# Inverse roots of the norms as one GpSimd power instruction, and a rope step of VectorE placed later

## The chip, the cores and the metric

The program runs on one core of a Trainium2 chip. The metric is the device time of one execution in microseconds (us), the median of several runs. TensorE (PE) multiplies matrices into PSUM, VectorE (DVE), ScalarE (ACT) and GpSimd (POOL) do elementwise work, and SyncE (SP) issues most of the loads. Each engine works through its own queue of instructions in order; an instruction that waits for another engine holds up everything behind it in its queue.

## The reference

Two layers of a decoder trunk on 256 tokens of width 1024. Each layer has three token mixers side by side, then a SwiGLU block and a gated embedding; each part begins with an RMSNorm.

```
def rmsnorm(x, g):
    y = xf * lax.rsqrt(jnp.mean(xf * xf, axis=-1, keepdims=True) + EPS)
    return (y * g)
per layer:
  h = rmsnorm(x); z = h @ W_in              # split into q, k, v, ... of mixers A, B, C
  A: sparse attention, B: sliding window with sinks, C: latent attention
     (C: rmsnorm of the low-rank q and kv before their up-projections)
  q and k of A and B, part of q and k of C: rotated by cos/sin(position * frequency)
  x += (sum of sigmoid(h @ Wg_i) * (o_i @ Wp_i)) @ W_out
  x += SwiGLU(rmsnorm(x));  x += sigmoid(rmsnorm(x) @ W_pg) * (p @ W_pe)
out = rmsnorm(x)
```

Two things of it matter here: the inverse square root, one number for each token and norm (256 numbers for each of seven norms of x, 512 for each layer's two low-rank norms together), and the rope tables, sine and cosine of position times frequency, which are made once.

## The kernel before

The 256 tokens are two tiles of 128 (t = 0, 1), tokens on partitions. Every product with a weight is made by `lin` in three float32r matmuls (high part of the input by high and by low part of the weight, low part by high part). So each weight chunk of up to 1024 columns is loaded by SP (tile `raw`, four buffers), rounded by ScalarE into `wh`, and the remainder taken by VectorE into `wl` (`wl<-raw,wh`); six pairs `wh`, `wl` are held. A full chunk serves 12 matmuls of 128x512, six for each token tile.

A norm of x does not scale its input: `Norm.tr` (or `parts` at the start) transposes x on TensorE, VectorE multiplies by the gain (`xg`), ScalarE rounds to the high part and VectorE makes the low part (both in tile `hT`). ScalarE meanwhile sums the squares (`junk`, into `ssq`). The inverse root `nm.r[t]` is needed only when a finished product leaves PSUM: as the scale of ScalarE's instruction, or as half of it (`rh`) in tanh for a sigmoid. The function `newton` makes the root: GpSimd adds the two halves of `ssq` and EPS (tile `n0v` or `n1v`, for t = 0 or 1), VectorE makes a first guess on the bits (`n0y`, `n1y`), and GpSimd does three Newton steps of two instructions (`n0a`, `n0y`), or of four for the low-rank norms of C (`c0v`, `c0y`, `c0a`, two columns). Of the last norm, t = 1 alone runs on VectorE, and `finish` then multiplies the output tile `xf` by the root and sends it out.

The first products are the gate of C (`gc0`, chunks 0 to 3, evacuated into `gateC` with `rh`) and the low-rank projections (`g1`, chunks 4 to 7, evacuated into `zc` with `nm.r`, and transposed on TensorE soon after). `lin` has three PSUM banks and takes two for each product, so `g1` for t = 1 reuses the bank that `gateC` of t = 0 frees.

The order on each queue is fixed by the program: a planner (`Plan`) with estimated costs holds small steps back in a list (`W.push`) and emits them between matmuls when they are due. The rope angles are made on GpSimd at the start (`setup_rope`, `rope_parts`, `finish_rope`: tiles `ang`, `kq`, `kp`); `rope_rest` then has VectorE take the larger of the angle and its negative (`kq<-kq,ang`), GpSimd turn it into the cosine's argument, ScalarE take two sines (tile `cs`; each change to or from the sine loads a table) and GpSimd spread them (`tabs`). During the first product, `start_1` and `start_2` emit the second half of the norm's input.

Of the kernel before, what the change touches and what calls it, by code (L numbers as in the profile page):

```python
# [11 lines left out]
I32 = mybir.dt.int32  # L12
AF = mybir.ActivationFunctionType
ALU = mybir.AluOpType
# [3 lines left out]
P = 128  # L18
# [199 lines left out]
def build(tc, wst, xin, pin, posn, cst, lpar, fnorm, out):  # L218
# [13 lines left out]
    W = Plan()  # L232
    V, S, T, G = (Engine(W, n, e) for n, e in (("V", nc.vector), ("S", nc.scalar), ("T", nc.tensor), ("G", nc.gpsimd)))

    def sb(shape, dt=F32, name="t", tag=None, bufs=1, p=pool):
        W.clear(tag or name, bufs)
        p = low if (tag or name) in FIRST else p
        t = p.tile(shape, dt, name=name, tag=tag or name, bufs=bufs)
        W.alloc(t.tensor.name, tag or name, bufs)
        return t  # L240

    def ps(tag, name=None):
        n = {"lin": 3, "pv": 1}.get(tag, 2)
        W.clear("ps" + tag, n)
        t = pp.tile([P, 512], F32, name=name or tag, tag=tag, bufs=n)
        W.alloc(t.tensor.name, "ps" + tag, n)
        return t
# [54 lines left out]
    def split_to(n):  # L302
        st["goal"] = max(st["goal"], n)
        feed()
# [101 lines left out]
    def small(n, name, bufs=2, dt=F32):  # L406
        return sb([P, n], dt, name=name, bufs=bufs)

    def transpose(o, i):
        T.transpose(o, i, ident)  # L410
# [8 lines left out]
    rope_t = {}  # L419
# [16 lines left out]
    def rope_parts(parts):  # L436
        ang, kq = rope_t["ang"], rope_t["kq"]
        kp = sb([P, 2, 48], name="kp", tag="kall", bufs=3)
        for bits in parts:
            rest = rope_t["rest"]  # L440
            part = rest if bits is None else math.floor(rest * 2 ** bits) / 2 ** bits
            rope_t["rest"] = rest - part
            G.tensor_scalar(out=kp, in0=kq, scalar1=-float(np.float32(part)), scalar2=None, op0=ALU.mult)
            G.tensor_tensor(out=ang, in0=ang, in1=kp, op=ALU.add)

    def finish_rope():
        rope_parts((27, None))
        ang, kq = rope_t["ang"], rope_t["kq"]
        pif = float(np.nextafter(np.float32(math.pi), np.float32(0)))
        G.tensor_scalar(out=ang, in0=ang, scalar1=pif, scalar2=-pif, op0=ALU.min, op1=ALU.max)  # L450
        G.tensor_scalar(out=kq, in0=ang, scalar1=-1.0, scalar2=None, op0=ALU.mult)
        W.push([kq], lambda: rope_rest(kq, ang), 0.2, [ang])

    def rope_rest(kq, ang):
        cs = sb([P, 2, 2, 48], name="cs", tag="dup0")
        V.tensor_tensor(out=kq, in0=kq, in1=ang, op=ALU.max)
        G.tensor_scalar(out=kq, in0=kq, scalar1=-1.0, scalar2=float(math.pi / 2), op0=ALU.mult, op1=ALU.add)

        def sin():
            S.activation(out=cs[:, 0], in_=kq, func=AF.Sin)  # L460
            S.activation(out=cs[:, 1], in_=ang, func=AF.Sin)
            W.push([cs], lambda: setup_tabs(cs))
        W.push([kq], sin, 0.2, [ang])

    def setup_tabs(cs):
        for i in range(2):
            for t in range(2):
                G.tensor_copy(out=tabs[:, t, 64 * i:64 * i + 64].rearrange("p (a b) -> p a b", a=2),
                              in_=cs[:, i, t, None, 0:32].to_broadcast([P, 2, 32]))
                G.tensor_copy(out=tabs[:, t, 128 + 32 * i:160 + 32 * i].rearrange("p (a b) -> p a b", a=2),  # L470
                              in_=cs[:, i, t, None, 32:48].to_broadcast([P, 2, 16]))
        ready_set.add("tabs")


    def newton(ssq, n, tag, G=G):

        v, y, a = small(n, tag + "v"), small(n, tag + "y"), small(n, tag + "a")
        one, two = ssq if isinstance(ssq, tuple) else (ssq, None)
        if two is None:
            G.tensor_scalar(out=v, in0=one, scalar1=EPS, scalar2=None, op0=ALU.add)  # L480
        else:
            G.tensor_scalar(out=v, in0=one, scalar1=two, scalar2=EPS, op0=ALU.add, op1=ALU.add)
        V.tensor_scalar(out=y.bitcast(I32), in0=v.bitcast(I32), scalar1=-0.5, scalar2=float(0x5F3759DF),
                        op0=ALU.mult, op1=ALU.add)
        G.tensor_scalar(out=v, in0=v, scalar1=-0.5, scalar2=None, op0=ALU.mult)
        for _ in range(3):
            if n == 1:
                G.tensor_scalar(out=a, in0=y, scalar1=y, scalar2=v, op0=ALU.mult, op1=ALU.mult)
                G.tensor_scalar(out=y, in0=a, scalar1=1.5, scalar2=y, op0=ALU.add, op1=ALU.mult)
            else:  # L490
                G.tensor_tensor(out=a, in0=y, in1=y, op=ALU.mult)
                G.tensor_tensor(out=a, in0=a, in1=v, op=ALU.mult)
                G.tensor_scalar(out=a, in0=a, scalar1=1.5, scalar2=None, op0=ALU.add)
                G.tensor_tensor(out=y, in0=y, in1=a, op=ALU.mult)
        return y

    def split_evac(src_ps, n, hi, lo, then, gain=None):

        s3 = src_ps[:, :n * P].rearrange("p (a b) -> p a b", a=n)
        if gain is not None:  # L500
            xg = sb([P, 4, P], name="xg")
            V.tensor_tensor(out=xg[:, :n], in0=s3, in1=gain[:, :, None].to_broadcast([P, n, P]), op=ALU.mult)
            s3 = xg[:, :n]
        S.copy(out=hi, in_=s3)

        def rest():
            V.tensor_tensor(out=lo, in0=s3, in1=hi.bitcast(F32), op=ALU.subtract)
            then()
        W.push([hi], rest, 0.0, [s3, lo])
# [3 lines left out]
    def finish(t, r):  # L513

        for g, c in enumerate([slice(0, 512), slice(512, 1024)] if t == 0 else [slice(0, 384), slice(384, 1024)]):
            o = xf[t][:, c]
            if g and t:
                V.tensor_scalar(out=o, in0=o, scalar1=r, scalar2=None, op0=ALU.mult)
            else:
                S.activation(out=o, in_=o, func=AF.Copy, scale=r)  # L520
            (nc.sync if g or not t else nc.scalar).dma_start(out=out[0, t * P:(t + 1) * P, c], in_=o)
        sent.append(t)
# [3 lines left out]
    class Norm:  # L526
# [55 lines left out]
            return o  # L582

        def fin(self, t, i=1):
            self.r[t] = newton((self.ssq[t][:, 0:1], self.ssq[t][:, i:i + 1]), 1, f"n{t}",
                               V if self.last and t else G)
            if self.last:
                if t:
                    finish(t, self.r[t])
                return  # L590
            self.rh[t] = small(1, f"rh{t}")
            G.tensor_scalar(out=self.rh[t], in0=self.r[t], scalar1=0.5, scalar2=None, op0=ALU.mult)
# [17 lines left out]
    def layer(l, nm, nxt):  # L610
# [12 lines left out]
        rc = [None, None]  # L623
        rcs = [small(1, f"rcs{t}") for t in range(2)]

        def ev_g1(t, b):
            zc = sb([P, 512], name="zc")
            S.activation(out=zc, in_=b, func=AF.Copy, scale=nm.r[t])
            s2 = small(2, f"s2{t}")
            for i in range(2):  # L630
                junk = sb([P, 512], BF16, name="junk")
                S.activation(out=junk[:, :256], in_=zc[:, 256 * i:256 * i + 256], func=AF.Square,
                             scale=1.0 / 16, accum_out=s2[:, i:i + 1])

            def tr():
                tb = ps("tr")
                for k in range(4):
                    transpose(tb[:, k * P:(k + 1) * P], zc[:, k * P:(k + 1) * P])
                split_evac(tb, 4, cTh[:, :, t * P:(t + 1) * P], cTl[:, :, t * P:(t + 1) * P],
                           lambda: flags.add(f"cT{t}"), lp[:, L_CN:L_CN + 4])  # L640
                rc[t] = newton(s2, 2, f"c{t}")
                G.tensor_scalar(out=rcs[t], in0=rc[t][:, 0:1], scalar1=float(96 ** -0.5), scalar2=None,
                                op0=ALU.mult)
            W.push([zc], tr)
# [641 lines left out]

    setup_rope()
    finish_rope()

    def parts(t, g):  # L1290
# [14 lines left out]
    def split(i):  # L1305
        if st["split"] == i:
            st["split"] += 1
            upper(i)
        return late.get(i, lambda: None)
# [9 lines left out]
    def start_2():  # L1319
        w3 = split(3)  # L1320
        lo = parts(1, 1)
        w3()
        lo()
        w4 = split(4)
        nm.square(0, 1)
        w4()
        nm.square(1, 1)
        W.push([], setup_masks, 20.0)
        split_to(HLB)

# [116 lines left out]
```

## Time and profile before

| | |
|---|---|
| median of 3 runs | 974.86 us (974.83 to 976.6) |
| profiled execution, its own time | 975.02 us |
| its span, first to last instruction | 973.3 us |
| TensorE busy | 955.2 us (98%), granted clock 0.997 |
| VectorE, ScalarE, GpSimd busy | 668.7, 555.5, 105.1 us |

The profiled execution is 0.16 us above the median and 1.7 us longer than its span. TensorE is busy nearly throughout; its idle time lies in the first 35 us, at a few places of some tenths, and after its last matmul. Busy times of TensorE contain pipelining: a 128x512 matmul is shown with about 0.39 us, but the next one starts 0.23 us after it.

### The profile page before, as it was taken

Reading aid. Unit: us, or ns where it says so; the run is one execution under the profiler, and the core shown is the slowest. Engines: PE = TensorE matmul, PEld = TensorE weight load, DVE = VectorE, ACT = ScalarE, POOL = GpSimd, SP = SyncE. Lnnn points to the kernel's source line nnn. Section 1 sums busy time; section 2 is a strip of 40 time slices with the busy share of each in tenths; the row PEclk is TensorE's granted clock in tenths of the full one; section 3 lists DMA queues with packets and bytes.
Section 4 is the critical chain, followed back from the end, with each engine's and each line's share of the span. In section 5 each row is a group of like instructions: output and inputs, shape, how many; then the busy total and the mean of one; then the engine's idle time right before and its main releaser. Section 6 shows DMA issues by size and latency. Waiting matters only on the chain.

```text
span 973.3 us, 13708 instructions
## 1 busy us (share of the span) xinstructions
PE 955.2 (98%) x4915; PEld 784.0 (81%) x4915; DVE 668.7 (69%) x1070; ACT 555.5 (57%) x1013; POOL 105.1 (11%) x224
## 2 busy tenths in 40 slices
PE   8899999999999999999999999999999999999996
PEld 5688888777888888888878898877788888888885
DVE  5697688658776666645767868876786766665555
ACT  5668767565554444543555686666655544444443
POOL 6700000000030000000454000000001200000032
PEclk9999999999999999999999999999999999999998
DMA  7556634434555655556454664343445555555551
GB/s 262 163 168 203 214 95 145 153 106 142 171 184 186 192 198 182 177 190 195 156 174 148 205 200 158 117 166 130 127 140 167 195 188 191 195 183 184 185 173 44
DMA packets 46596, 164.29 MB, mean 169 GB/s; under 512 B 5504, under 2 KB 5760, under 8 KB 46528
## 3 DMA queue, kind: packets, MB, share of 16 engines
q1 hardware_dynamic: 45648, 161.80, 50.5%
q0 software_dynamic: 448, 1.30, 0.5%
q8 instruction: 39, 0.64, 0.3%
q10 hardware_dynamic: 432, 0.32, 0.1%
q14 instruction: 29, 0.24, 0.1%
HBM read 162.35 MB, written 1.05 MB: 168 GB/s over the span
## 4 chain that ended last, share of the span: by engine, by line
PE 93%; POOL 3%; DVE 2%; issue 1%; ACT 1%; ACTq 0%; DVEq 0%; POOLq 0%
PE lin L214 77%; PE tr L214 6%; PE sc L214 5%; PE pv L214 3%; PE hidps L214 2%; POOL kp L214 0%; POOL n1a L214 0%; POOL n0a L214 0%; DVE wl L214 0%; ACT wh L214 0%; POOL ang L214 0%; DVE um L214 0%; POOL kq L214 0%; POOL n0y L214 0%; POOL n0v L214 0%
## 5 line engine op out<-in xcount | busy, mean ns | idle before, releaser
L214 PE MATMUL lin<-wh,hT 128*128 128x512 f32 (+2 forms) x1600 | 512.9, 389 | 1.6 <-DVE hT L214 0.9
L214 DVE TENSOR_TENSOR wl<-raw,wh 128x1024 fp32r<-128x1024 f32 (+2 forms) x308 | 369.0, 1209 | 91.0 <-ACT wh L214 85.4
L214 ACT CAST wh<-raw 128x1024 fp32r<-128x1024 f32 (+2 forms) x308 | 317.0, 1037 | 133.3 <-PE lin L214 125.4
L214 PEld LDWEIGHTS lin<-wh,hT 128*128 128x128 f32 x1600 | 297.0, 188 | 58.5 <-DVE hT L214 1.7
L214 PE MATMUL lin<-wl,hT 128*128 128x512 f32 (+2 forms) x800 | 305.2, 381 | 2.5 <-DVE wl L214 2.5
L214 PEld LDWEIGHTS lin<-wl,hT 128*128 128x128 f32 x800 | 150.8, 189 | 28.2 <-DVE wl L214 3.2
L214 PE MATMUL lin<-wh,hd 128*128 128x512 f32 x352 | 110.9, 392 | 0.0
L214 PEld LDWEIGHTS lin<-wh,hd 128*128 128x128 f32 x352 | 66.1, 188 | 13.6
L214 POOL TENSOR_SCALAR n0v<-ssq 128x1 f32<-128x1 f32 x7 | 2.5, 358 | 686.8 <-ACT junk L214 686.8
L214 PE MATMUL lin<-wl,hd 128*128 128x512 f32 x176 | 68.5, 389 | 0.0
L214 PE MATMUL lin<-wh,oT 128*128 128x512 f32 x192 | 64.6, 397 | 0.0
L214 ACT ACTIVATE th<-lin,rh 128x256 f32<-128x256 f32 (+1 forms) x52 | 26.2, 504 | 66.3 <-PE lin L214 63.2
L214 ACT ACTIVATE p<-sc,negm 128x256 f32<-128x256 f32 (+1 forms) x128 | 52.7, 426 | 2.7 <-DVE negm L214 2.7
L214 DVE SCALAR_TENSOR_TENSOR th<-th,lin 128x256 f32<-128x256 f32 x44 | 18.4, 419 | 49.9 <-ACT th L214 49.9
L214 DVE TENSOR_REDUCE negm<-sc 128x2 f32<-128x512 f32 (+1 forms) x48 | 33.0, 687 | 27.3 <-PE sc L214 27.1
L214 ACT COPY pT<-tr 128x512 f32<-128x512 f32 x48 | 28.1, 584 | 36.2 <-PE tr L214 36.2
L214 PEld LDWEIGHTS lin<-wh,oT 128*128 128x128 f32 x192 | 36.1, 188 | 7.7 <-issue 0.8
L214 PE MATMUL lin<-wh,mT 128*128 128x512 f32 x128 | 41.4, 395 | 0.0
L214 PEld LDWEIGHTS lin<-wl,hd 128*128 128x128 f32 x176 | 33.1, 188 | 6.7
L214 PE MATMUL lin<-wl,oT 128*128 128x512 f32 x96 | 37.5, 390 | 0.0
L214 ACT CAST hd<-tr 128x256 fp32r<-128x256 f32 x44 | 16.2, 369 | 33.5 <-PE tr L214 33.5
L214 DVE TENSOR_TENSOR p<-p,sm 128x512 f32<-128x512 f32 x48 | 33.2, 692 | 2.1
(226 smaller groups left out, 1070.7 us busy)
## 6 DMA issues: line engine op xcount, KB each, us to landing
raw<-wst SPq DMA_DIRECT2D x296, 512.0 KB, 4.0
raw<-wst SPq DMA_DIRECT2D x8, 312.0 KB, 2.8
raw<-wst SPq DMA_DIRECT2D x4, 384.0 KB, 3.1
x<-xin SPq DMA_DIRECT2D x4, 256.0 KB, 5.9
w<-lpar POOLq DMA_DIRECT2D x2, 256.0 KB, 3.0
pr<-pin POOLq DMA_DIRECT2D x2, 256.0 KB, 3.5
fn<-fnorm SPq DMA_DIRECT2D x1, 512.0 KB, 3.3
out<-xf SPq DMA_DIRECT2D x2, 256.0 KB, 2.0
```

Of the source, the lines that this page charges most:

```text
L214: return fn(*a, **k)
```

## The change

The function `newton` becomes `rsqrt`: GpSimd adds EPS as before and then raises the sum to the power of -0.5 in one tensor_tensor instruction whose second input is a small tile `half` that is filled with -0.5 at the start. The guess on VectorE and the Newton steps are gone, for all norms. The last norm's t = 1 goes through GpSimd as well, where before it stayed on VectorE. The step `rope_rest` is no longer pushed with a due time; it is kept in `rope_t["last"]` and emitted in `start_2`, after the last sum of squares.

```
-        W.push([kq], lambda: rope_rest(kq, ang), 0.2, [ang])
+        rope_t["last"] = lambda: rope_rest(kq, ang)
...
-    def newton(ssq, n, tag, G=G):
+    half = sb([P, 2], name="half")
+    G.memset(half, -0.5)
+    def rsqrt(ssq, n, tag):
-        v, y, a = small(n, tag + "v"), small(n, tag + "y"), small(n, tag + "a")
+        v, y = small(n, tag + "v"), small(n, tag + "y")
...
-        V.tensor_scalar(out=y.bitcast(I32), in0=v.bitcast(I32), scalar1=-0.5, scalar2=float(0x5F3759DF),
-                        op0=ALU.mult, op1=ALU.add)
-        G.tensor_scalar(out=v, in0=v, scalar1=-0.5, scalar2=None, op0=ALU.mult)
-        for _ in range(3):
-            if n == 1:
-                G.tensor_scalar(out=a, in0=y, scalar1=y, scalar2=v, op0=ALU.mult, op1=ALU.mult)
-                G.tensor_scalar(out=y, in0=a, scalar1=1.5, scalar2=y, op0=ALU.add, op1=ALU.mult)
-            else:
...
+        G.tensor_tensor(out=y, in0=v, in1=half[:, 0:n], op=ALU.pow)
...
-            self.r[t] = newton((self.ssq[t][:, 0:1], self.ssq[t][:, i:i + 1]), 1, f"n{t}",
-                               V if self.last and t else G)
+            self.r[t] = rsqrt((self.ssq[t][:, 0:1], self.ssq[t][:, i:i + 1]), 1, f"n{t}")
...
-                rc[t] = newton(s2, 2, f"c{t}")
+                rc[t] = rsqrt(s2, 2, f"c{t}")
...
         nm.square(1, 1)
+        rope_t["last"]()
         W.push([], setup_masks, 20.0)
```

VectorE's queue in the first 30 us, before. The first row is the low part of the third of four pieces of the norm's input, the next `xg` belongs to the fourth.

```order
L214 TENSOR_TENSOR hT<-xg,hT 128x4x128
L214 TENSOR_TENSOR kq<-kq,ang 128x96
L214 TENSOR_TENSOR xg<-tr,lp 128x512
L214 TENSOR_TENSOR wl<-raw,wh 128x1024
L214 TENSOR_TENSOR hT<-xg,hT 128x4x128
L214 TENSOR_TENSOR wl<-raw,wh 128x1024
L214 TENSOR_SCALAR n0y<-n0v 128x1
L214 TENSOR_SCALAR n1y<-n1v 128x1
L214 CAST identb<-con 128x128
L214 CAST identr<-con 128x128
L214 CAST masks<-mload 128x256
L214 TENSOR_TENSOR wl<-raw,wh 128x1024 x5
```

The same place after:

```order
L214 TENSOR_TENSOR hT<-xg,hT 128x4x128
L214 TENSOR_TENSOR xg<-tr,lp 128x512
L214 TENSOR_TENSOR wl<-raw,wh 128x1024
L214 TENSOR_TENSOR hT<-xg,hT 128x4x128
L214 TENSOR_TENSOR wl<-raw,wh 128x1024
L214 TENSOR_TENSOR kq<-kq,ang 128x96
L214 TENSOR_TENSOR wl<-raw,wh 128x1024
L214 CAST identb<-con 128x128
L214 CAST identr<-con 128x128
L214 CAST masks<-mload 128x256
L214 TENSOR_TENSOR wl<-raw,wh 128x1024 x4
```

The rope step has moved behind the fourth `xg`, two weight remainders and the last low part of the norm's input; the two guesses are gone.

GpSimd's queue from the last rope instructions on, after. Before, nine instructions stood for each root and its half in place of these three.

```order
L214 TENSOR_SCALAR ang<-ang 128x96
L214 TENSOR_SCALAR kq<-ang 128x96
L373 DMA w_217<-lpar 128x512
L214 TENSOR_SCALAR kq<-kq 128x96
L214 TENSOR_SCALAR n0v<-ssq_135 128x1
L214 TENSOR_TENSOR n0y<-n0v,half 128x1
L214 TENSOR_SCALAR rh_314<-n0y 128x1
L214 TENSOR_SCALAR n1v<-ssq_136 128x1
L214 TENSOR_TENSOR n1y<-n1v,half 128x1
L214 TENSOR_SCALAR rh_329<-n1y 128x1
```

The roots still stand behind the rope instruction that waits for VectorE (`kq<-kq`), so its later place moves them too.

ScalarE's queue from the end of the sums of squares to `zc`, before:

```order
L214 ACTIVATE junk,ssq_134<-x_106 128x512
L214 ACT_TABLE_LOAD
L214 ACTIVATE cs<-kq 128x96
L214 ACTIVATE cs<-ang 128x96
L214 CAST wh<-raw 128x1024 x3
L214 ACT_TABLE_LOAD
L214 ACTIVATE gateC<-lin,rh_322 128x512
L214 ACTIVATE gateC<-lin,rh_345 128x512
L214 CAST wh<-raw 128x1024 x2
L214 ACTIVATE zc<-lin,n0y 128x512
```

and after:

```order
L214 ACTIVATE junk,ssq_136<-x_106 128x512
L214 CAST wh<-raw 128x1024 x2
L214 ACT_TABLE_LOAD
L214 ACTIVATE cs<-kq 128x96
L214 ACTIVATE cs<-ang 128x96
L214 CAST wh<-raw 128x1024
L214 ACT_TABLE_LOAD
L214 ACTIVATE gateC<-lin,rh_314 128x512
L214 ACTIVATE gateC<-lin,rh_329 128x512
L214 CAST wh<-raw 128x1024 x2
L214 ACTIVATE zc<-lin,n0y 128x512
```

Two of the three weight roundings now stand ahead of the sines and their table load. On TensorE and SP the order of the work is the same in both kernels.

## Rows read from the trace of the kernel before

**Rows 1.** The page: busy times (part 1), and the chain that ended last, by engine (part 4).

```profile
PE 955.2 (98%) x4915; PEld 784.0 (81%) x4915; DVE 668.7 (69%) x1070; ACT 555.5 (57%) x1013; POOL 105.1 (11%) x224
...
PE 93%; POOL 3%; DVE 2%; issue 1%; ACT 1%; ACTq 0%; DVEq 0%; POOLq 0%
```

**Rows 2.** Timeline of TensorE, 17 to 35 us: start, duration, instruction, and in brackets the idle time before it and what ended it.

```profile
17.78 0.39 PE L214 MATMUL lin<-wh,hT 128*128 128x512 f32 x1
18.76 0.50 PE L214 MATMUL lin<-wh,hT 128*128 128x512 f32 x1 [0.60 <-ACT hT L214]
...
19.85 0.74 PE L214 MATMUL lin<-wh,hT 128*128 128x512 f32 x2 [0.35 <-DVE hT L214]
...
26.58 0.50 PE L214 MATMUL lin<-wl,hT 128*128 128x512 f32 x1 [1.18 <-DVE wl L214]
26.92 0.62 PE L214 MATMUL lin<-wh,hT 128*128 128x512 f32 x2
...
31.70 0.39 PE L214 MATMUL lin<-wh,hT 128*128 128x512 f32 x1
34.36 0.66 PE L214 MATMUL tr<-con,zc 128*128 128x128 f32 x4 [2.28 <-ACT zc L214]
```

**Rows 3.** Groups of instructions of TensorE in the window 18.7 to 32.2 us, with their counts, busy time, mean ns, and idle time before them.

```profile
L214 PE MATMUL lin<-wh,hT 128*128 128x512 f32 x32 | 10.3, 398 | 1.0 <-ACT hT L214 0.6 <-DVE hT L214 0.4
L214 PE MATMUL lin<-wl,hT 128*128 128x512 f32 x16 | 6.3, 397 | 1.2 <-DVE wl L214 1.2
```

**Rows 4.** Timeline of VectorE, 14 to 29 us.

```profile
14.27 0.75 DVE L214 TENSOR_TENSOR hT<-xg,hT 128x512 fp32r<-128x512 f32 x1
17.20 0.26 DVE L214 TENSOR_TENSOR kq<-kq,ang 128x96 f32<-128x96 f32 x1 [2.18 <-POOL kq L214]
17.38 0.68 DVE L214 TENSOR_TENSOR xg<-tr,lp 128x512 f32<-128x512 f32 x1
...
19.71 1.22 DVE L214 TENSOR_TENSOR wl<-raw,wh 128x1024 fp32r<-128x1024 f32 x1
...
24.77 0.16 DVE L214 TENSOR_SCALAR n1y<-n1v 128x1 int32<-128x1 int32 x1 [3.47 <-POOL n1v L214]
...
25.31 3.49 DVE L214 TENSOR_TENSOR wl<-raw,wh 128x1024 fp32r<-128x1024 f32 x3
```

**Rows 5.** Timeline of ScalarE, 18 to 34 us.

```profile
18.09 0.62 ACT L214 CAST hT<-xg 128x512 fp32r<-128x512 f32 x1 [3.53 <-DVE xg L214]
...
21.06 1.28 ACT L214 ACT_TABLE_LOAD   x1
...
22.72 2.93 ACT L214 CAST wh<-raw 128x1024 fp32r<-128x1024 f32 x3
25.66 1.28 ACT L214 ACT_TABLE_LOAD   x1
26.95 0.69 ACT L214 ACTIVATE gateC<-lin,rh 128x512 f32<-128x512 f32 x1
31.16 0.69 ACT L214 ACTIVATE gateC<-lin,rh 128x512 f32<-128x512 f32 x1 [3.51 <-POOL rh L214]
...
33.62 0.69 ACT L214 ACTIVATE zc<-lin,n0y 128x512 f32<-128x512 f32 x1
```

**Rows 6.** Timeline of GpSimd, 17 to 37 us.

```profile
17.12 0.62 POOL L373 DMA_DIRECT2D w<-lpar  x1
...
20.38 0.73 POOL L214 TENSOR_SCALAR n0v<-ssq 128x1 f32<-128x1 f32 x1 [2.33 <-ACT junk L214]
...
23.78 0.26 POOL L214 TENSOR_SCALAR n0y<-n0a,n0y 128x1 f32<-128x1 f32 x1
...
25.53 3.31 POOL L214 TENSOR_SCALAR n1a<-n1y,n1v 128x1 f32<-128x1 f32 x1
...
30.91 0.21 POOL L214 TENSOR_SCALAR rh<-n1y 128x1 f32<-128x1 f32 x1
...
36.21 0.20 POOL L214 TENSOR_TENSOR c0a<-c0y 128x2 f32<-128x2 f32 x1
```

**Rows 7.** Timeline at the start of the second layer: VectorE, then TensorE.

```profile
499.55 0.15 DVE L214 TENSOR_SCALAR n1y<-n1v 128x1 int32<-128x1 int32 x1 [3.09 <-POOL n1v L214]
499.62 0.68 DVE L214 TENSOR_TENSOR hT<-xg,hT 128x512 fp32r<-128x512 f32 x1
...
499.47 0.39 PE L214 MATMUL lin<-wl,hT 128*128 128x512 f32 x1
500.36 0.73 PE L214 MATMUL lin<-wh,hT 128*128 128x512 f32 x2 [0.50 <-DVE hT L214]
```

**Rows 8.** Timeline of the end: GpSimd, VectorE, ScalarE.

```profile
962.09 0.29 POOL L214 TENSOR_SCALAR n0v<-ssq 128x1 f32<-128x1 f32 x1 [8.46 <-ACT junk L214]
...
966.84 0.21 DVE L214 TENSOR_SCALAR n1v<-ssq 128x1 f32<-128x1 f32 x1 [0.18 <-ACT junk L214]
...
969.13 0.55 DVE L214 TENSOR_SCALAR xf<-xf,n1y 128x640 f32<-128x640 f32 x1
...
966.62 0.19 ACT L214 ACTIVATION_READ_ACCUMULATOR junk<-x 128x1 f32 x1
967.27 1.33 ACT L214 ACTIVATE xf<-xf,n0y 128x512 f32<-128x512 f32 x2 [0.47 <-POOL n0y L214]
969.13 0.62 ACT L214 ACTIVATE xf<-xf,n1y 128x384 f32<-128x384 f32 x1 [0.53 <-DVE n1y L214]
```

More of the change, by code (lines that the diff above doesn't have):

```diff
@@ L482, in newton @@
             G.tensor_scalar(out=v, in0=one, scalar1=two, scalar2=EPS, op0=ALU.add, op1=ALU.add)
-        V.tensor_scalar(out=y.bitcast(I32), in0=v.bitcast(I32), scalar1=-0.5, scalar2=float(0x5F3759DF),
-                        op0=ALU.mult, op1=ALU.add)
-        G.tensor_scalar(out=v, in0=v, scalar1=-0.5, scalar2=None, op0=ALU.mult)
-        for _ in range(3):
-            if n == 1:
-                G.tensor_scalar(out=a, in0=y, scalar1=y, scalar2=v, op0=ALU.mult, op1=ALU.mult)
-                G.tensor_scalar(out=y, in0=a, scalar1=1.5, scalar2=y, op0=ALU.add, op1=ALU.mult)
-            else:
[L491 to L494, printed above, removed]
+        G.tensor_tensor(out=y, in0=v, in1=half[:, 0:n], op=ALU.pow)
         return y
```

## The prediction

> **What bounds the kernel now.** I read the page's busy times and chain first, then TensorE's waits and timeline, then what each wait hangs on. TensorE is busy 98% and makes up 93% of the chain that ended last [rows 1], so a step on another engine counts only where TensorE stands still for it, or after its last matmul. GpSimd holds 3% of the chain: about 29 us of 973 in which its small steps ended last, though it is busy 11%. TensorE's idle times after the ramp are few. In the head there are four: 0.60 and 0.35 us for the last piece of the norm's input, 1.18 for a weight remainder, 2.28 for `zc` [rows 2]. One of 0.50 stands at the start of layer 2 [rows 7]. The rest of the gain can only lie in the tail, behind the last matmul [rows 8].
>
> What each head wait hangs on: VectorE finishes `hT` at 14.27 + 0.75 = 15.02 us, then stands 2.18 us at the rope step, which waits for GpSimd, with the fourth `xg` behind it [rows 4]. ScalarE idles 3.53 us for that `xg` [rows 5], and TensorE waits for both parts of `hT`. Next, VectorE stands 3.47 us at `n1y`, the guess for t = 1, because GpSimd first finishes all of t = 0; three `wl` queue behind it and run only at 25.31 [rows 4], and TensorE meets the first of them. Last, `n1a` takes 3.31 us beside those three `wl` [rows 6], so `rh` of t = 1 comes at 30.91 + 0.21, `gateC` starts at 31.16, two weight roundings follow, and `zc` starts only at 33.62 [rows 5].
>
> **The head, summed.** Idle times of a pipelined engine understate what is lost, so I count matmuls. From 26.92 to 31.70 us TensorE issues 21 matmuls without a wait, one each 0.228 us [rows 2]. From the one at 17.78 to the transpose of `zc` at 34.36 there are 49: that one and the 48 of the window [rows 3]. 49 x 0.228 = 11.2, so without a stall the transpose would start at 28.95. Lost: 5.4 us. That is all the head can give.
>
> Does the change give it? The rope step goes behind the `xg`, so `xg` starts at 15.02 instead of 17.38, 2.36 earlier. ScalarE, which idles there, shifts by as much: its sums of squares, which end at 21.06 before [rows 5], end at 18.7. It then does two roundings (three take 2.93, so about 1.95), the table load 1.28, the sines and one rounding (1.45 together), the second load 1.28: 24.65. Both `gateC` and the two roundings behind them, then `zc`, took from 31.16 to 34.31, 3.15 us [rows 5]. That gives about 28.5 with `zc` done, 0.45 before TensorE wants it. The remainders follow the roundings and have no guess ahead of them, so the wait for `wl` goes. What is late next is this ScalarE chain itself, with 0.45 us to spare.
>
> The condition is that GpSimd has `rh` of t = 0 by 24.65 and of t = 1 by some 25.7. It turns to the roots once the rope instruction behind VectorE's step is done, about 19.8: the step has to wait for the fourth `wl` (about 18.6), and GpSimd's weight transfer of 0.62 [rows 6] stands between. One root is now `n0v` 0.29 when undisturbed [rows 8], 0.73 beside a `wl` [rows 6], one power instruction of X, and `rh` 0.21, with 0.09 between instructions. If `n0v` is held by a `wl` until 21.2, `rh` of t = 1 comes at 21.2 + 1.2 + 2X. With one hold of about 1.2 behind a `wl` more (1.22 each [rows 4]), that makes 25.7 at X = 1.0. Each tenth beyond costs TensorE two tenths.
>
> **X**, the power instruction, is not in the trace. Nearest below: a two-input GpSimd instruction on 128x2 takes 0.20 [rows 6]. It cannot be cheaper than a multiply of the same form. Far above: the whole chain that it replaces for t = 0, from 20.38 to 23.78 + 0.26, 3.7 us [rows 6], if the engine's own routine does as much as the kernel wrote out. I take 0.4, near the lower row, because one element per partition is almost all fixed cost; both ends stay for the range.
>
> Of the 5.4 us I count 5.0: 0.4 for a hold that eats the spare time.
>
> What the shared access to SBUF does shows in `n1a`: 3.31 us beside three back-to-back `wl` [rows 4, 6] where undisturbed instructions of its kind take 0.3. The Trainium skill's "SBUF — State Buffer" (Who interferes with whom) says that a VectorE instruction with two SBUF inputs and a GpSimd instruction exclude each other for the whole instruction. It speaks against the new place of the step: `wl`, `hT`, `wl` would now run beside GpSimd's last rope instructions. By that rule those wait until VectorE itself stops at the rope step, about 1.3 us later than I have it, and the head gives some 4.5 instead of 5.0.
>
> **Layer 2.** VectorE stands 3.09 us at `n1y` with `hT` behind it; TensorE's issue at 499.47 + 0.23 = 499.70 slips to 500.36, 0.66 [rows 7], and the two matmuls after a stall take about 0.1 more (0.34 from 26.58 to 26.92 for one [rows 2]). No guess, no stall: 0.75. The other norms' roots are off TensorE's path: no wait of it names them. They become cheaper and cost nothing.
>
> **The tail.** Before, the accumulator is read by 966.81, eight small VectorE instructions follow, and both last multiplies start at 969.13 [rows 8]. After, GpSimd takes about 0.1 to start, `n1v` 0.29, 0.1, X, 0.05: 967.35 + X. But ScalarE multiplies t = 0 first, 1.33 us, now from 966.84 as that root is long done (its sum starts at 962.09 and no guess is waited for), until 968.17. Its last piece then starts at 968.17 instead of 969.13: 0.96 less while X is under 0.8, and X + 967.35 - 969.13 more or less beyond. The output transfers follow each other closely, so I count 0.9.
>
> **Sum.** 5.0 + 0.75 + 0.9 = 6.65 off the profiled execution's 975.02: 968.4 us. The median of the runs is 0.16 lower, so beside it the forecast is 968.2.
>
> **Rivals.**
>
> Held roots. GpSimd's steps are caught by `wl` more than once, or X is 1 to 2 us. For: the six instructions of GpSimd until `rh` of t = 1 run while VectorE catches up on four `wl`, and `n1a` shows how long one can be held [rows 6]. Against: each root now touches SBUF in three instructions, not nine. At X = 2 the head loses 2.0, the tail gives -0.2 instead of 0.9: 975.0 - 3.4 - 0.75 + 0.2 = 971.1.
>
> The first power instruction alone is dear. For it the "GPSIMD Engine Reference" of the Trainium skill (Instruction dispatch) gives about 6 us for the first call to a freshly loaded kernel; no row here shows a first power instruction, and by that figure `rh` of t = 1 is 4.3 late and the time about 972.3, an estimate. By rows: if the first takes 3.7 and the next 0.4, `rh` of t = 1 comes at 21.2 + 1.2 + 4.1 + 1.2 = 27.7, 2.0 late; the head gives 3.4 and the time is 970.0.
>
> Given back. TensorE comes 5 us earlier to weights that are not split faster; then the head's gain goes in later waits for `wl`, leaving layer 2 and the tail: 973.4. For: one of the four waits was for `wl`. Against: it came from a guess in the queue, and VectorE and ScalarE are busy 69% and 57% [rows 1].
>
> Slower. The power routine is slow each time. At X = 4.2, `rh` of t = 1 is 6.4 us late: the head turns from 5.4 gained to 1.0 lost. The tail's `n1y` comes at 971.55, 2.4 late; layer 2 still gives 0.75. 975.0 + 1.0 + 2.4 - 0.75 = 977.7. It decides from X about 3.3, where the head still gives 0.8 and layer 2 0.75, and the tail loses 1.5. For: nothing shows the price, and the tail now hangs on it directly. Against: one instruction would have to cost about what the whole chain does that it replaces.
>
> **How the numbers follow.** Forecast 0.64, held roots 0.13, dear first use 0.08, given back 0.06, slower 0.09. A measurement of this kernel can tell about 0.2%, 2 us. The first three cases are faster, given back is within it: faster 0.85, same 0.06, slower 0.09. The range: its low end is the whole head, layer 2 and a tail of the full 1.4 that VectorE's piece could gain (975.0 - 5.4 - 0.75 - 1.4 = 967.4), less 0.6 for the count; its high end lies a little beyond X = 2. 966.8 to 972.0.
>
> **What would show it.** In the new profile `xg` starts near 15.0, TensorE has no wait from 17 to 29 us and transposes `zc` near 29.0; the wait at 500 is gone, with TensorE about 5 us earlier from 40 us on to the end; the power instruction reads 0.2 to 0.8; ScalarE's last `xf` follows the first two without a gap. I am wrong if the power instruction takes above 1 us, if `gateC` waits for `rh` again, or if TensorE shows new waits for `wl` between 30 and 60 us.

## The result and the profile after

| | before | after |
|---|---|---|
| median on the same chip | 975.73 us (974.83 to 976.7, 4 runs) | 967.4 us (967.17 to 968.79, 4 runs) |
| ratio to before | | 0.9918, 95% interval 0.9905 to 0.9932 |
| profiled execution, its span | 975.02, 973.3 | 968.79, 967.0 |

The changed kernel is 0.8% faster. Its profiled execution is the slowest of its four runs: TensorE's granted clock fell for a few microseconds in the ramp, which is told of in the last section. A second profile of the same kernel, of a run of 967.44 us with a span of 965.6, has the clock at 1.00 throughout, and the rows below are from that one (called e6) unless said otherwise.

Page of the changed kernel, second profile (e6): span, busy times, and the chain that ended last.

```profile
span 965.6 us, 13566 instructions
...
PE 953.7 (99%) x4915; PEld 784.5 (81%) x4915; DVE 665.9 (69%) x1044; ACT 555.1 (57%) x1013; POOL 52.7 (5%) x101
...
PE 95%; POOL 2%; ACT 1%; DVE 1%; issue 1%; ACTq 0%; POOLq 0%
```

Against [rows 1], GpSimd has 123 instructions fewer and half the busy time. It has not left the chain: it holds 2% of it, all in the first 26 us, where its rope steps and then the two roots still lead up to the second `gateC`. Of the layer 2 roots, which stood in the chain before (`n0a` from 493.77 us), none is left in it. TensorE's own busy time hardly moves: the work is the same, and idle time went.

TensorE's waits in e6, whole run: what it waited for, us in total, times, the longest.

```profile
PE pv L1276 <- DVE wrm L214: 1.4, 1, 1.4
PE lin L214 <- DVE wl L214: 1.2, 1, 1.2
PE sc L214 <- ACT kTC L214: 0.7, 2, 0.4
PE tr L214 <- ACT dup L214: 0.4, 2, 0.2
```

The four head waits of [rows 2] (for both parts of `hT`, for `wl`, for `zc`) and the one of [rows 7] are no longer in the list. The `wl` wait that is left is that of the ramp, at 10.24 us; the kernel before had it too.

Timelines of e6: TensorE at `zc`, then VectorE, GpSimd and ScalarE at the same place and, in their last rows, in the tail (start, duration, instruction, idle time before it and what ended it).

```profile
29.09 0.66 PE L214 MATMUL tr<-con,zc 128*128 128x128 f32 x4
```

```profile
15.18 0.69 DVE L214 TENSOR_TENSOR xg<-tr,lp 128x512 f32<-128x512 f32 x1
...
17.72 1.28 DVE L214 TENSOR_TENSOR wl<-raw,wh 128x1024 fp32r<-128x1024 f32 x1
19.35 0.26 DVE L214 TENSOR_TENSOR kq<-kq,ang 128x96 f32<-128x96 f32 x1 [0.34 <-POOL kq L214]
19.82 1.22 DVE L214 TENSOR_TENSOR wl<-raw,wh 128x1024 fp32r<-128x1024 f32 x1 [0.22 <-ACT wh L214]
...
21.51 1.21 DVE L214 TENSOR_TENSOR wl<-raw,wh 128x1024 fp32r<-128x1024 f32 x1
23.48 1.23 DVE L214 TENSOR_TENSOR wl<-raw,wh 128x1024 fp32r<-128x1024 f32 x1 [0.76 <-ACT wh L214]
...
961.18 0.55 DVE L214 TENSOR_SCALAR xf<-xf,n1y 128x640 f32<-128x640 f32 x1 [1.22 <-POOL n1y L214]
```

```profile
18.01 1.30 POOL L214 TENSOR_SCALAR kq<-ang 128x96 f32<-128x96 f32 x1
...
19.91 1.26 POOL L214 TENSOR_SCALAR kq<-kq 128x96 f32<-128x96 f32 x1
21.27 0.42 POOL L214 TENSOR_SCALAR n0v<-ssq 128x1 f32<-128x1 f32 x1
21.77 1.38 POOL L214 TENSOR_TENSOR n0y<-n0v,half 128x1 f32<-128x1 f32 x1
...
23.57 1.30 POOL L214 TENSOR_SCALAR n1v<-ssq 128x1 f32<-128x1 f32 x1
24.96 0.57 POOL L214 TENSOR_TENSOR n1y<-n1v,half 128x1 f32<-128x1 f32 x1
25.61 0.23 POOL L214 TENSOR_SCALAR rh<-n1y 128x1 f32<-128x1 f32 x1
...
960.59 0.56 POOL L214 TENSOR_TENSOR n1y<-n1v,half 128x1 f32<-128x1 f32 x1
```

```profile
24.76 0.69 ACT L214 ACTIVATE gateC<-lin,rh 128x512 f32<-128x512 f32 x1
25.88 0.69 ACT L214 ACTIVATE gateC<-lin,rh 128x512 f32<-128x512 f32 x1 [0.42 <-POOL rh L214]
...
28.35 0.69 ACT L214 ACTIVATE zc<-lin,n0y 128x512 f32<-128x512 f32 x1
...
959.91 0.19 ACT L214 ACTIVATION_READ_ACCUMULATOR junk<-x 128x1 f32 x1
960.01 1.32 ACT L214 ACTIVATE xf<-xf,n0y 128x512 f32<-128x512 f32 x2
961.23 0.60 ACT L214 ACTIVATE xf<-xf,n1y 128x384 f32<-128x384 f32 x1
```

Against [rows 4], `xg` starts at 15.18 instead of 17.38, and VectorE's long stands (2.18 at the rope step, 3.47 at the guess) have become 0.34 at the rope step and 0.76 for a rounding. Against [rows 5], the second `gateC` starts at 25.88 instead of 31.16, and `zc` at 28.35 instead of 33.62. Against [rows 8], the last pieces of `xf` start 1.1 us behind the end of the accumulator's reading (960.10), where it was 2.3.

### The profile page after: what moved, and what is told of

Read it like the earlier page. It is cut to its first block, busy times and chain, and to the rows that moved or that the text cites. A ratio compares the mean times of both kernels' runs of the same rounds, so it can differ in the third digit from the quotient of the medians.

```text
span 967.0 us, 13566 instructions
## 1 busy us (share of the span) xinstructions
PE 954.5 (99%) x4915; PEld 785.3 (81%) x4915; DVE 665.5 (69%) x1044; ACT 555.2 (57%) x1013; POOL 51.0 (5%) x101
## 4 chain that ended last, share of the span: by engine, by line
PE 97%; DVE 1%; ACT 1%; DMA 1%; issue 0%; ACTq 0%; DVEq 0%
PE lin L214 81%; PE tr L214 7%; PE sc L214 5%; PE pv L214 3%; PE hidps L214 2%; DMA lp<-lpar 1%; DVE wl L214 0%; DVE um L214 0%; ACT xf L214 0%; DVE khA L214 0%; DVE U L214 0%; ACT dup L214 0%; ACT ctok L214 0%; ACT kTC L214 0%; ACT gat L214 0%
## 5 line engine op out<-in xcount | busy, mean ns | idle before, releaser
L214 DVE TENSOR_TENSOR xg<-tr,lp 128x512 f32<-128x512 f32 x28 | 19.3, 689 | 26.3 <-PE tr L214 20.9
```

Source lines behind the costliest of these rows:

```text
L214: return fn(*a, **k)
```

## The experiments

Ten kernels ran: four undo or isolate one part, one undoes the tail, two are the two kernels again, and three ask about differences that the first profiles left.

**e1: the rope step alone.** The kernel before, with only the rope step moved.

```
-        W.push([kq], lambda: rope_rest(kq, ang), 0.2, [ang])
+        rope_t["last"] = lambda: rope_rest(kq, ang)
...
+        rope_t["last"]()
```

> Newton steps kept, only the rope step comes later. Theory (the roots' chain on GpSimd sets the head): the two waits for hT go, but the guess for t = 1 still waits for the whole of t = 0 and holds the weight remainders, and rh of t = 1 still comes near 30 us, so TensorE transposes zc near 33.2 instead of 34.4. Time 973.8, about 1 us less than before. Rival (VectorE's stall at the rope step is what holds the head): the transpose near 31.5 and 971.5 or less.

Measured: 973.54 us (972.75 to 973.64, 6 runs), ratio 0.9969 (0.9957 to 0.9980). TensorE, then ScalarE, of the 972.75 us run:

```profile
25.06 0.50 PE L214 MATMUL lin<-wl,hT 128*128 128x512 f32 x1 [1.70 <-DVE wl L214]
31.90 0.66 PE L214 MATMUL tr<-con,zc 128*128 128x128 f32 x4 [1.33 <-ACT zc L214]
```

```profile
29.63 0.69 ACT L214 ACTIVATE gateC<-lin,rh 128x512 f32<-128x512 f32 x1 [4.42 <-POOL rh L214]
30.22 1.04 ACT L214 CAST wh<-raw 128x1024 fp32r<-128x1024 f32 x1
31.15 0.69 ACT L214 ACTIVATE zc<-lin,n0y 128x512 f32<-128x512 f32 x1
```

The two waits for `hT` are gone. That for `wl` grows from 1.18 to 1.70 and ScalarE's for `rh` from 3.51 to 4.42, because the guesses and the Newton steps are where they were: `n1a` again takes 3.31 us. The transpose of `zc` comes 2.46 us earlier than in [rows 2], of which 0.46 is a ramp that happened to be shorter in this run (first matmul with `wl` at 9.90 against 10.36). So the head gains 2.0 where the theory had 1.2, and the transpose, at 31.90, lies nearer to the rival's 31.5. The theory holds for the gate: the second `gateC` is 1.53 earlier, 1.07 without the ramp. The other 0.94 comes from ScalarE's order, which neither expectation had: one weight rounding, not two, now stands between that `gateC` and `zc`. The whole is 2.1 shorter in this run (974.9, where the kernel before stands with the clock at full, less 972.75). The other five runs, at 973.45 to 973.64, show a slightly lower mean clock (0.995 to 0.997 against 0.998); where it fell is not shown.

**e2: the power instructions alone.** The changed kernel with the rope step where it was.

```
-        rope_t["last"] = lambda: rope_rest(kq, ang)
+        W.push([kq], lambda: rope_rest(kq, ang), 0.2, [ang])
...
-        rope_t["last"]()
```

> Power instruction, rope step where it was before. Theory: VectorE still stands 2.2 us at the rope step, TensorE loses the 0.75 and 0.5 us for hT and nothing else, and transposes zc near 30.4; layer 2 and the tail gain as in the changed kernel. Time about 968.8, 1.4 above the changed kernel. Rival (the two parts need each other, since ScalarE's roundings, table loads and gates all come 2.4 us later): zc near 31.5, time 970 or more.

Measured: 969.48 us (969.32 to 970.2), ratio 0.9930 (0.9918 to 0.9942). TensorE and GpSimd:

```profile
31.03 0.66 PE L214 MATMUL tr<-con,zc 128*128 128x128 f32 x4 [0.58 <-ACT zc L214]
```

```profile
21.17 0.57 POOL L214 TENSOR_TENSOR n0y<-n0v,half 128x1 f32<-128x1 f32 x1
```

The waits for `hT` stay (0.60 and 0.35), that for `zc` shrinks from 2.28 to 0.58. The theory had no wait there; place and time lie between the two expectations, as ScalarE's gates and roundings come 2 us later than in e6 (first `gateC` at 26.81 against 24.76), which is the rival's reason. Here the kernel's very first power instruction met no long VectorE instruction and took 0.57, as the later ones do: a dear first use is refuted. The two parts alone give 2.1 (e1's fastest run; 1.4 by its median) and 5.4 (974.9 - 969.48), together 7.5 (974.9 - 967.4). In the head, counted from the first matmul with `wl`, they give 2.00 and 3.18, and 5.15 together; the sum comes out, though 0.94 of the 2.00 hangs on e1's order.

**e3: the guess without its chain.** The changed kernel with VectorE's guess put back, into a tile that nothing reads. It tells whether the instruction in VectorE's queue costs, or the Newton chain ahead of it.

```
+        u = small(n, tag + "u")
+        V.tensor_scalar(out=u.bitcast(I32), in0=v.bitcast(I32), scalar1=-0.5, scalar2=float(0x5F3759DF),
+                        op0=ALU.mult, op1=ALU.add)
```

> The changed kernel, and VectorE still makes the guess on n0v and n1v in its queue, into a tile that nothing reads. Theory (the guess costs only because a long chain of GpSimd stands ahead of n1v): n1v is ready near 21.6 us, the remainders behind the guess are at most 2 us later and still in time; layer 2 shows no wait. Time 967.3 to 967.6, as the changed kernel. Rival (the round trip to VectorE itself costs): the wait for wl of over 1 us is back and 0.75 in layer 2, time 969.2.

Measured: 968.05 us (967.46 to 968.09, 4 runs), ratio 0.9913 (0.9899 to 0.9926). VectorE, then TensorE:

```profile
20.59 0.15 DVE L214 TENSOR_SCALAR n0u<-n0v 128x1 int32<-128x1 int32 x1 [1.04 <-POOL n0v L214]
21.96 0.15 DVE L214 TENSOR_SCALAR n1u<-n1v 128x1 int32<-128x1 int32 x1 [1.22 <-POOL n1v L214]
```

```profile
29.57 0.66 PE L214 MATMUL tr<-con,zc 128*128 128x128 f32 x4 [0.34 <-ACT zc L214]
```

VectorE stands 2.26 us, TensorE only 0.34, and the time rises by 0.6 over e6's 967.43. The expectation of no cost in the head was missed by that: SP's weight transfers wait for the remainders, and ScalarE's last rounding before `zc` waits 0.98 us for such a transfer, which it does not in e6. Layer 2 shows no wait, as expected. So the wait in VectorE's queue cost mainly because what it waited for stood behind all of t = 0's Newton steps.

**e4: the chain without the guess.** The changed kernel with three Newton steps put back on GpSimd behind the power instruction.

```
+        a = small(n, tag + "a")
+        G.tensor_scalar(out=v, in0=v, scalar1=-0.5, scalar2=None, op0=ALU.mult)
+        for _ in range(3):
+            if n == 1:
+                G.tensor_scalar(out=a, in0=y, scalar1=y, scalar2=v, op0=ALU.mult, op1=ALU.mult)
+                G.tensor_scalar(out=y, in0=a, scalar1=1.5, scalar2=y, op0=ALU.add, op1=ALU.mult)
...
```

> The changed kernel with the three Newton steps on GpSimd behind the power instruction: the old length of the chain without the guess on VectorE. Theory (length): rh of t = 1 near 30, zc near 33, TensorE waits about 4 us at its transpose; no wait for wl and none in layer 2; the tail 3 us longer. Time about 974.3. Rival (the guess in VectorE's queue was the cost): the head stays within 1 us of the changed kernel and only the tail pays, 970.5.

Measured: 977.44 us (976.68 to 977.8, 11 runs), ratio 1.0009 (1.0000 to 1.0019); 3.1 more than expected. ScalarE, TensorE, then a window (columns: window, its length, busy us of PE, PEld, DVE, ACT and POOL with counts, granted clock, DMA share, GB/s):

```profile
31.20 0.69 ACT L214 ACTIVATE gateC<-lin,rh 128x512 f32<-128x512 f32 x1 [3.43 <-POOL rh L214]
```

```profile
34.41 1.11 PE L214 MATMUL tr<-con,zc 128*128 128x128 f32 x4 [4.92 <-ACT zc L214]
...
42.76 0.60 PE L214 MATMUL tr<-con,zc 128*128 128x128 f32 x4
```

```profile
35.00:37.00 2.00, 2.00 (x7) 1.65 (x6) 1.50 (x3) 1.91 (x4) 1.30 (x3) 0.50 0.79 205
```

`zc` is 5.3 us later than in e6 (34.41 against 29.09), at the place where the kernel before has it: the chain's length alone brings that wait back. The expectation missed what follows: behind the 4.92 us idle the clock reads 0.50, the lower level (1.2 GHz), and the second transpose of `zc` is 7.7 us later than in e6 (42.76 against 35.06), 2.4 more than the first. The tail is 2.6 longer as well (10.39 us from the last matmul's start to the end, against 7.81). 7.7 + 2.6 = 10.3, of 10.0 by the times.

**e5: the tail alone.** The changed kernel with the last norm's t = 1 as it was, a guess and Newton steps on VectorE.

```
+    def newton_v(ssq, tag):
...
-            self.r[t] = rsqrt((self.ssq[t][:, 0:1], self.ssq[t][:, i:i + 1]), 1, f"n{t}")
+            two = (self.ssq[t][:, 0:1], self.ssq[t][:, i:i + 1])
+            self.r[t] = newton_v(two, f"n{t}") if self.last and t else rsqrt(two, 1, f"n{t}")
```

> The changed kernel, but the last norm's root for t = 1 is made by a guess and Newton steps on VectorE, as before. Theory (the length of the last root sets the end): both last multiplies start 2.3 us after the sum of squares is read instead of 1.05, so the time is about 1.2 us above the changed kernel with the same ramp, 968.5. Rival (the output transfers or ScalarE's two other pieces set the end): within 0.3 us of it, 967.5.

Measured: 968.39 us (968.25 to 968.44, 5 runs), ratio 0.9925 (0.9912 to 0.9939). ScalarE:

```profile
960.08 1.32 ACT L214 ACTIVATE xf<-xf,n0y 128x512 f32<-128x512 f32 x2
962.50 0.62 ACT L214 ACTIVATE xf<-xf,n1y 128x384 f32<-128x384 f32 x1 [1.11 <-DVE n1y L214]
```

ScalarE finishes t = 0 and then waits 1.11 us for the root, which it does not in e6. The tail is 8.74 us against 7.81; by the times the root on GpSimd is worth 968.39 - 967.43 = 0.96.

**e6 and e7: both kernels again**, unchanged, for a second profile of each.

> The changed kernel once more. Theory (the 1.5 us between its own runs is the granted clock in the ramp): a profile of a run near 967.3 shows clock 1.00 from 8 to 16 us, the transpose of zc at 28.7 to 29.0, no wait of TensorE between 17 and 29 us; one of a run near 968.8 shows about 0.5 for 3 to 4 us there and the transpose near 30.5. Rival (the runs differ elsewhere): the transpose is at the same place in both.

> The kernel before once more. Theory as for the changed kernel: a run near 974.9 shows clock 1.00 in the ramp, one near 976.6 about 0.5 for 3 to 4 us before 16 us; part of what is lost there comes back, as the stalls behind it are shorter. Rival: the 1.7 us lie elsewhere, in the head's waits or in layer 2.

Measured: e6 967.43 us (967.14 to 967.48, 4 runs); e7 975.73 (974.97 to 977.14, 10 runs), ratio 1.0002 (0.9993 to 1.0011). e7's profile is of a 976.29 us run. TensorE at the first `zc`, and windows behind it:

```profile
34.06 1.12 PE L214 MATMUL tr<-con,zc 128*128 128x128 f32 x4 [2.27 <-ACT zc L214]
```

```profile
33.00:35.00 2.00, 0.94 (x5) 0.94 (x6) 1.87 (x2) 1.94 (x7) 0.00 (x0) 0.74 0.18 26
35.00:37.00 2.00, 2.00 (x6) 1.61 (x6) 1.71 (x3) 1.56 (x4) 1.18 (x2) 0.50 0.71 197
37.00:39.00 2.00, 2.00 (x9) 1.61 (x9) 1.13 (x3) 1.05 (x1) 1.67 (x6) 0.91 0.57 154
```

The stall is the same as in [rows 2], but here the clock then falls to 0.50 and the second transpose of `zc` starts at 41.57, although the first came 0.3 earlier than in the first profile of this kernel, which has the second at 40.33. So for e7 the rival holds: in the ramp the clock reads 1.00, and the loss lies in the head, behind the wait for `zc`. For e6 the theory held: 1.00 in the ramp and the transpose at 29.09. The kernel before thus has two kinds of execution; beside e9 and e10 ten of its 21 runs read 974.82 to 975.24 and eleven 976.49 to 976.79.

**e8: the ramp kept warm.** The changed kernel with two more warm-up matmuls and five idle ones between the first two matmuls of the first product.

```
+                    if c0 == 0 and t == 0 and k == 0:
+                        warm(5)
...
-WARM = (7, 4, 4)
+WARM = (7, 6, 4)
```

> The changed kernel with seven more idle matmuls in the ramp, two before the second transpose and five between the first product's first two matmuls, where TensorE waits 0.5 and 1.3 us. Theory (the clock falls after those waits): the clock stays 1.00 in all runs, all lie within 0.3 us of 967.3. Rival (the fall has another cause, or the added matmuls delay the first product): the spread of 1.5 us stays, or all runs are 0.3 to 0.6 slower.

Measured: 967.27 us (967.23 to 967.37, 4 runs), ratio 0.9914 (0.9900 to 0.9928). The ramp's idle of 1.27 us becomes 0.19 and all runs lie within 0.14 us. But of the eight runs of the unchanged version only one (968.79) was slower, so four even ones do not show that the ramp's idle was its cause. No gain over e6 can be told.

**e9: the tile alone.** The kernel before with the small tile `half` allocated and filled, and read by nothing.

```
+    half = sb([P, 2], name="half")
+    G.memset(half, -0.5)
```

> The kernel before, with the small tile half allocated and filled, and read by nothing. Its only effect is that what is allocated after it in SBUF lies elsewhere. In the second block (SwiGLU) the transposes of h come every 5.714 us in both profiles of the kernel before and in that of the one with only the rope step moved, and every 5.693 in all that have the tile. Theory (the place of the tiles): 5.693 here, and about 0.9 us less in all (44 such steps of 0.021): 974.0 where the clock holds, 975.5 where it falls. Rival (it comes with the power instruction): 5.714 and no change.

Measured: 974.49 us (974.19 to 976.03, 11 runs, of which eight up to 974.67 and three from 975.98), ratio 0.9989 (0.9980 to 0.9998). Two successive rounds on TensorE in the SwiGLU block, of e9 and of the kernel before:

```profile
293.94 0.38 PE L214 MATMUL tr<-con,h 128*128 128x128 f32 x2
...
299.63 0.38 PE L214 MATMUL tr<-con,h 128*128 128x128 f32 x2
```

```profile
293.80 0.38 PE L214 MATMUL tr<-con,h 128*128 128x128 f32 x2
...
299.51 0.38 PE L214 MATMUL tr<-con,h 128*128 128x128 f32 x2
```

With the tile one round of the block takes 5.69 us, without it 5.71, though the instructions are the same. The spacing is 5.69 in every kernel here that has `half` and 5.71 in every one that has not. The eight faster runs all lie below the lowest of the kernel before in the same round, 974.82; between the middles of the two faster groups lie 0.5 us, where 0.9 was expected. The rounds give what was expected, 0.42 us in each layer, but 0.17 and 0.15 go again in the attention parts of layers 1 and 2. So some 0.5 us of the change's gain comes with the tile and not with the work. That the place of the later tiles does it is what is left, not what was shown: besides it the edit adds one short memset on GpSimd, near 3 us.

**e10: no idle ahead of `zc`.** The kernel before with 24 transposes of the identity on TensorE while it waits for the first `zc`. It asks whether the stall is what brings the clock down.

```
+                if l == 0 and t == 0:
+                    for k in range(24):
+                        nc.tensor.transpose(tb[:, 0:P], ident, ident)
```

> The kernel before, with 24 transposes of the identity ahead of those of zc in the first layer, into the bank that these overwrite: TensorE works 2.1 us where it stood 2.3. Theory (the clock falls after that stall in the slower executions of the kernel before): the clock is 1.00 from 33 to 39 us in all of them, and all lie near 974.9 to 975.2. Rival (another cause): two groups 1.6 us apart as before.

Measured: 975.05 us (974.96 to 975.29, 11 runs), ratio 0.9991 (0.9983 to 1.0000). TensorE, then a window:

```profile
31.80 2.78 PE L639 MATMUL tr<-con 128*128 128x128 f32 x24
34.42 0.60 PE L214 MATMUL tr<-con,zc 128*128 128x128 f32 x4
```

```profile
35.00:37.00 2.00, 2.00 (x11) 1.63 (x10) 1.57 (x4) 2.00 (x5) 1.26 (x4) 1.00 0.79 197
```

The transpose of `zc` is no earlier, but none of the eleven runs reads above 975.29: with the engine busy the slower kind of execution is gone. The idle ahead of `zc` caused the fall.

## Why the prediction was right

The forecast was 968.2, the time is 967.4, in the range. The main line holds; the terms, by the two profiles whose clock is at full (spans 973.3 and 965.6, 7.7 us apart):

| step | predicted | measured |
|---|---|---|
| head, to the transpose of `zc` | 5.0 of 5.4 | 5.15 |
| layer 2 | 0.75 | 0.85 |
| tail | 0.9 | 1.0 |
| not foreseen | | 0.55 with the tile `half`, 0.12 in the ramp |

The foreseen terms were forecast at 6.65 and measured 7.0. The 0.67 that no term foresaw did not make the hit: without it the time would lie still nearer to 968.2.

**The head.** `zc` is transposed at 29.09 instead of 34.36, 5.27 earlier, of which 0.12 is the ramp's (the first matmul with `wl` at 10.24 against 10.36 us; e7, the kernel before again, has 10.06, so this is scatter). From there the lead is carried to the end: at the score matmuls of C it is 5.26 (95.56 against 100.82 us). So the rival "given back" fell: no wait for `wl` came in its place. The parts went as said. `xg` started at 15.18 (said: near 15.0), the second table load of ScalarE ended at 24.75 (24.65), no TensorE wait is left from 17 to 29. One reading was loose: the 3.15 us from 31.16 to 34.31 hold one `gateC`, not both. With the other's 0.69 added, 24.65 does give the 28.5 that the working uses.

**X.** It was sized at 0.4 and measured 0.57 where nothing held it, in e2's head and in the tail. The mark "wrong if the power instruction takes above 1 us" did show, as the first one took 1.38, but that is a hold (below) and not its price. The slower side, which needed 3.3, is far off, and so is the dear first use: no program's first power instruction took over 1.71. The Trainium skill's "GPSIMD Engine Reference" (Instruction dispatch) has some 6 us for the first call to a freshly loaded kernel; no run here shows such a time, nor whether the power operation has to be loaded at all.

**Held roots.** This rival was half right, and 0.4 was put aside for it. GpSimd's step `kq<-kq`, 0.28 in the kernel before, took 1.26 beside a `wl`; the first root took 1.38 beside the next and `n1v` 1.30 beside a third: three holds, where the working reckoned with an `n0v` done at 21.2 (it was done at 21.69) and one hold more. `rh` of t = 1 was done at 25.84 against the 25.7 asked for, `gateC` waited 0.42 for it, and `zc` ended at 29.04 instead of 28.5. By the count that is 0.24 late: the transpose would have started at 17.68 + 49 x 0.228 = 28.85 and did at 29.09. The mark "wrong if `gateC` waits for `rh` again" was set too strictly: the 0.45 us of spare time took up most of that wait. The rule in the Trainium skill's "SBUF — State Buffer" (Who interferes with whom), that a VectorE instruction with two SBUF inputs and a GpSimd instruction that reads SBUF exclude each other for a whole instruction, agrees with each of these rows. What was worked out from it came only in part. GpSimd's `kq<-ang` took 1.30 instead of the 0.45 it has in the kernel before, and its last rope step was done at 21.17, 1.4 later than the 19.8 of the working (1.3 by the rule). But VectorE stood only 0.34 at the rope step, and the head did not fall to 4.5: the working had room for X = 1.0, and two power instructions of 0.57 left 0.9 of it.

**Layer 2.** The stall of [rows 7] is gone, and between the end of the first SwiGLU block and the transpose of `zc` in layer 2 the lead grows by 0.85 us (5.56 to 6.41). The other norms' roots show in no wait of TensorE, as said.

**The tail.** ScalarE's last piece follows its first two directly, at 961.23; the root is there at 961.15, just in time. Both engines thus start their last pieces together, and the span after the last matmul's start shrinks from 8.83 to 7.81. e5 confirms the size by undoing it alone: 0.96.

**The unforeseen part.** No step of the prediction had the tile `half` moving other tiles. The lead grows by 0.42 in each of the two SwiGLU blocks (5.13 to 5.55, 6.23 to 6.65), less the 0.13 and 0.18 that go again in the attention parts of layers 1 and 2, about 0.55. e9 has gains and losses alike without the rest of the change (0.42, 0.17 and 0.15). And a saving not in the forecast: in those executions of the kernel before in which the clock falls behind the stall at `zc`, the change also takes away that fall, 1.6 us more (976.6 against 975.0). The forecast was set beside runs of both kinds, so part of the ratio is this.

## What to carry to other kernels

A short chain on a slow engine can hold up a saturated one through queues: follow each wait to the engine that ended last, count matmuls at their issue spacing to see what the stall really cost, and ask whose spare time comes next. An instruction that waits in another engine's queue costs according to the chain ahead of it (e3 against e4), so shortening the chain and moving the waiting step are worth trying apart; here 5.4 and up to 2.1 us. And compare kernels with an idle copy of every added tile before a gain of a few tenths is put down to the work.

## What the runs showed of the hardware

**TensorE's clock behind a short stall.** After the same 2.3 us of idle ahead of `zc` the granted clock of the kernel before fell to 0.50, the lower level (1.2 GHz), in one profile and stayed at 1.00, the upper (2.4 GHz), in the other. Two groups of times 1.6 us apart say how often: the slower holds 13 of 16, 6 of 15 and 11 of 21 runs in three rounds, and none of e10's eleven, where TensorE worked through that idle time. After 4.92 us (e4) all eleven times are at or above 976.68, and the one profile reads 0.50. The price at 2.3 us was about 1.6 us, and the clock came back to 1.00 once the matmuls ran on (0.91 from 37 to 39 us in e7). In the first profile of the changed kernel it fell in the ramp, after idle times of 0.52, 0.27 and 1.27 us:

```profile
11.60:13.50 1.90, 1.90 (x8) 1.66 (x7) 1.51 (x3) 1.57 (x4) 1.75 (x3) 0.52 0.91 328
13.50:15.30 1.80, 1.80 (x8) 1.31 (x7) 1.80 (x2) 1.48 (x2) 1.63 (x3) 0.56 0.74 280
```

```profile
30.51 0.60 PE L214 MATMUL tr<-con,zc 128*128 128x128 f32 x4
```

There the transpose of `zc` stands at 30.51 instead of 29.09: that is the 1.4 us between the first profile and the other runs. Why it fell in one of eight executions stays open; e5's profile has idle times of 0.59 and 1.21 us in its ramp and reads 1.00 there.

**The place of tiles.** An unread tile of two columns changed the pace of the SwiGLU block's matmuls by 0.4% (5.71 to 5.69 us a round), 0.5 us in all with what the attention parts lose. Why stays open; no run moved single tiles.

**The power instruction.** One power of 128x1 on GpSimd took 0.56 to 0.58 us when undisturbed, against 0.2 to 0.34 for a multiply, and up to 1.71 beside a `wl`.
